# Cosine-similarity attention on one core: a third chunk of exponentials computed without ScalarE, moment statistics for Q in half of the norm groups, joint products

## The chip, the core and the metric

The kernel runs on one core of a Trainium2 chip. The metric is device time in microseconds (us), median of several runs. The core's engines work side by side, each through its own list of instructions in order, and meet at semaphores: TensorE (PE in the profile; PEld is its weight load), VectorE (DVE), ScalarE (ACT), GpSimd (POOL), and SyncE (SP), which here only issues DMAs.

## The reference

```python
Q, K, V: (8, 12, 512, 64) float32, tau = 0.1
Q_norm = Q / (norm(Q, axis=-1) + 1e-10)
K_norm = K / (norm(K, axis=-1) + 1e-10)
scores = einsum('bhqd,bhkd->bhqk', Q_norm, K_norm) / tau
weights = exp(scores - max(scores)); weights = weights / (sum(weights) + 1e-10)
return einsum('bhqk,bhkd->bhqd', weights, V)
```

Scores lie between -10 and 10, so the kernel leaves the maximum out; it gets the sum of a row's weights from a column of ones that stands beside V.

## The kernel before

The 96 heads are worked in 48 pairs of two. For a pair `s` (function `pair`, from L323, and `rest`, from L619) these operations are made, in names that the text below uses:

- **Loads** (L334, L339): Q, K and V of both heads, 128 partitions of 4 rows each. Q and K go to a ring of 15 buffers, V to one of 10.
- **Squares** (L366): GpSimd squares Q and K in one instruction of 128x1024, to bf16.
- **Sums of squares** (L393): TensorE multiplies the squares with a unit matrix, 16 matmuls of 64 columns that add up in PSUM (8 for Q, 8 for K), and VectorE reduces the 64 columns to 16 norms (L410). For the K of pairs in `BY_VECTOR`, and then the Q too, VectorE reduces the 128x512 squares itself (L418).
- **Inverse roots** (L442 to L473): for a norm group of pairs (`GROUPS`: one, two, then four pairs at a time, 19 groups) VectorE makes 1/sqrt in 8 or 9 small instructions.
- **Scaling** (L485): Q on VectorE; K on VectorE for the pairs in `K_ON_DVE`, on GpSimd for the others; 128x512 each.
- **Transposes** (L494): 8 on TensorE into one PSUM buffer, copied out by VectorE (L512).
- **Scores** (L633): for each of four chunks of 128 keys two matmuls of 512 columns, one for each head, that run beside each other on two halves of the array. Two PSUM buffers of 128x1024 take turns.
- **Exponentials** (L657): ScalarE, 128x1024 for a chunk, from PSUM to bf16.
- **Products** (L682): 32 matmuls of 65 columns with V (cast to bf16 by GpSimd, L665), in groups of four; head 0 into one PSUM bank, head 1 into another.
- **Outputs**: for each head VectorE takes the reciprocal of the four row sums (L701) and multiplies (L703), and SP stores the pair (L707). The products of the next pair may only write a bank that has been read.

Two of the 192 chunks, chunk 3 of pairs 36 and 45 (`OFF`), do without ScalarE (`poly`, L554): TensorE writes the scores of one head at a time into the transposes' PSUM buffer, VectorE splits each value into an exponent that is a bf16 bit pattern (L573) and a rest (L575), and GpSimd makes a polynomial of the rest in six instructions of 128x1024 (L601 to L604).

The order on every engine is written out by hand in `ORDER` (L814): five lists of numbers, each the place of an operation in the program's list, in which a pair's operations stand together. Each operation also carries a kind and a due time, as a planner would use them, but nothing in the file reads them: the lists alone set the order. An operation waits for those that it needs (`needs`) and, its engine being in order, so does all that stands behind it.

Of the kernel before, what the change touches and what calls it, by code (L numbers as in the profile page):

```python
# [5 lines left out]
ALU = mybir.AluOpType  # L6
# [102 lines left out]
def bass_cosine_similarity_attention_kernel(  # L109
# [200 lines left out]
    def stats(s):  # L310
        return s >= STATS_FROM and group[s] not in NORM_ON_ACT

# [10 lines left out]
    def pair(s):  # L323
# [6 lines left out]
        for w, x in ((0, Q), (1, K)):  # L330
            if s == 0:
                for h in range(2):
                    P.add(("LD", 0, w, h), "act" if w else "sp", "ldh", -1000 + h,  [],
                          lambda e, w=w, x=x, h=h: e.dma_start(out=qk[iq][:, w, h], in_=src(x, s)[:, h]), slot=f"head{w}_{h}")  # L334
                continue
            P.add(("LD", s, w), "sp", "ld1" if s == 1 else "ld", s, [*([("SCL", 0, w, 0), ("SCL", 0, w, 1), ("SQ", 0, w, 0), ("SQ", 0, w, 1)] if s == R_QK else [key("SCL", s - R_QK, w), *((squares(s - R_QK, w) if w or not stats(s - R_QK) else [("RED", s - R_QK, 0)]) if s >= R_QK else [])])],
                  lambda e, w=w, x=x: e.dma_start(out=qk[iq][:, w], in_=src(x, s)),
                  slot=f"first{s}_{w}" if s <= 3 else f"qk{iq}")
# [195 lines left out]
    def last_step(s, c):  # L534
        return 5 if (s, c) in OFF_ON_POOL + OFF_ON_BOTH else 4
# [18 lines left out]
    def poly(s, c, at):  # L554
# [4 lines left out]
        a0, a1, a2, a3, a4 = POLY_K if here else POLY  # L559
# [39 lines left out]
        if (s, c) in OFF_ON_POOL:  # L599
            k = cc ** 0.5  # L600
            steps = [("pool", "yt", mul(w, z, z)), ("pool", "ys", add(w, w, a1, k)),  # L601
                     ("pool", "ys", lambda e: e.tensor_scalar(out=z, in0=z, scalar1=a2 * cc, scalar2=a3 * cc, op0=ALU.mult, op1=ALU.add)),
                     ("pool", "yt", mul(w, w, w)), ("pool", "yt2", lambda e: e.tensor_tensor(out=w, in0=w, in1=z, op=ALU.add)),
                     ("pool", "yt3", mul(e_, w, p2))]  # L604
# [146 lines left out]
POLY = (-186.9751803485176, 100772.4799431421, -50373599.073513225, 207520169.07623482, 3.565140779347853e-11)  # L751
OFF = {(36, 3): (36, 36), (45, 3): (45, 45)}
# [8 lines left out]
BY_VECTOR = (35, 39, 43, 47)  # L761
Q_ON_PE = ()
SUM_BOTH = (4, 5, 6, 7, 8, 9, 10, 11, 12, 13, 14, 15, 16, 17, 18, 19, 20, 21, 22, 23, 24, 25, 26, 27, 28, 29, 30, 31, 32, 33, 34, 36, 37, 38, 40, 41, 42, 44, 45, 46)
# [3 lines left out]
STATS_FROM = 99  # L767
# [6 lines left out]
JOINT = False  # L774
RCPJ = ()
JOINT_FROM = 0
OFF_ON_POOL = ((36, 3), (45, 3))
OFF_ON_BOTH = ()
X_ON_POOL = ()
K_ON_DVE = (1, 2, 3, 4, 9, 12, 15, 18, 21, 24, 27, 30, 33, 36, 39, 40, 42, 44, 46, 47)  # L780
# [29 lines left out]
def slack(s, most):  # L810
# [14 lines left out]
    ),  # L825
    "pool": (
# [113 lines left out]
```

## Time and profile before

| | before |
|---|---|
| device time, median of 3 runs | 189.33 us (188.67, 189.33, 189.76) |
| span of the profiled execution | 186.8 us |
| median less that span | 2.5 us |
| ScalarE busy | 180.2 us (96%) |
| TensorE matmuls busy, weight loads busy | 179.5 us (96%), 117.9 us (63%) |
| GpSimd busy | 165.7 us (89%) |
| VectorE busy | 159.9 us (86%) |
| granted TensorE clock | 1.000 |

The span runs from the first instruction to the last of the profiled execution; the device time has what lies around it as well. Busy is the time in which an engine has at least one instruction in work. Instructions of ScalarE and VectorE overlap with the next one of the same engine, so their durations add up to more than the busy time, and what one of them costs is the step from its start to the start of the next.

### The profile page before, as it was taken

The page shows a single profiled execution, that of the slowest core. Times are in us where ns is not written, and L with a number is a line of the kernel's source. Part 1 is how long each engine was busy: PE and PEld are TensorE (multiplying, and loading weights), DVE is VectorE, ACT ScalarE, POOL GpSimd, SP SyncE. Part 2 cuts the span into 40 slices and gives each one's busy share as a digit, 9 for nine tenths or more (in the row PEclk, how much of TensorE's full clock was granted, in tenths as well). Part 3 has the DMA queues.
Part 4 walks back from the last instruction along what each step waited for, and adds up shares of the span by engine and source line. Part 5 has one row for each costly group of instructions (what it writes and reads, how often), then busy time and mean ns, then how long its engine had stood idle before and what let it go on. Part 6 is the DMA issues. An engine that isn't in the chain of part 4 may idle for free.

```text
span 186.8 us, 7242 instructions
## 1 busy us (share of the span) xinstructions
PE 179.5 (96%) x3010; PEld 117.9 (63%) x3010; DVE 159.9 (86%) x523; ACT 180.2 (96%) x210; POOL 165.7 (89%) x147
## 2 busy tenths in 40 slices
PE   7889999999999999999999999999999999998993
PEld 2456766666667666666676666766656566555653
DVE  2789998987987978979889988999999999998664
ACT  5799999999999999999999999999999999999992
POOL 3799999999989998999999899999999999907940
PEclk9999999999999999999999999999999999999999
DMA  5999999999999877999999999999798731113135
GB/s 158 354 349 351 349 358 329 288 351 364 370 376 369 283 245 230 309 303 307 312 379 367 328 371 335 319 312 298 241 303 294 239 105 56 60 56 116 60 112 168
DMA packets 52447, 50.79 MB, mean 272 GB/s; under 512 B 3136, under 2 KB 52416, under 8 KB 52416
## 3 DMA queue, kind: packets, MB, share of 16 engines
q1 hardware_dynamic: 51984, 50.02, 81.8%
q8 instruction: 23, 0.38, 0.8%
q10 hardware_dynamic: 432, 0.33, 0.5%
q14 instruction: 8, 0.07, 0.1%
HBM read 37.75 MB, written 12.58 MB: 269 GB/s over the span
## 4 chain that ended last, share of the span: by engine, by line
ACT 92%; PE 3%; DVE 2%; DMA 1%; POOL 0%; issue 0%; DVEq 0%
ACT et L657 91%; DMA qk<-in_K_dram 1%; PE oops L682 1%; PE scps L633 1%; DVE xs L260 1%; DVE ob L732 0%; POOL sq L256 0%; PE tps L283 0%; ACT ys L432 0%; DVE qn L273 0%; DVE ob L703 0%; PE oops L401 0%; ACT nps L435 0%; PE oops L281 0%; DVE rd L730 0%
## 5 line engine op out<-in xcount | busy, mean ns | idle before, releaser
L657 ACT ACTIVATE et<-scps 128x1024 bf16<-128x1024 f32 (+1 forms) x191 | 173.8, 1155 | 0.3 <-PE scps L633 0.3
L366 POOL TENSOR_TENSOR sq<-qk 128x1024 bf16<-128x1024 f32 x44 | 82.8, 1895 | 0.6 <-DMA qk<-in_K_dram 0.6
L633 PE MATMUL scps<-qt 64*128 64x512 bf16 x380 | 74.5, 386 | 2.2 <-ACT et L657 1.0
L682 PE MATMUL oops<-vb,et 128*128 128x65 bf16 x1504 | 75.8, 194 | 0.1
L682 PEld LDWEIGHTS oops<-vb,et 128*128 128x128 bf16 x1504 | 57.0, 98 | 27.7 <-issue 21.9
L485 DVE TENSOR_TENSOR qn<-qk,nps 128x512 bf16<-128x512 f32 x67 | 44.2, 678 | 0.7 <-ACT nps L435 0.6
L703 DVE TENSOR_TENSOR ob<-oops,rd 128x256 f32<-128x256 f32 x94 | 39.5, 422 | 1.7 <-DVE ys L447 0.2
L512 DVE COPY qt<-tps 128x1024 bf16<-128x1024 bf16 x47 | 32.3, 687 | 3.9 <-PE tps L494 3.0
L494 PE MATMUL tps<-ident,qn 128*128 128x128 bf16 x376 | 34.3, 220 | 0.6 <-DVE qn L485 0.6
L485 POOL TENSOR_TENSOR qn<-qk,rk 128x512 bf16<-128x512 f32 x27 | 28.1, 1045 | 2.6 <-DVE rk L443 1.7
L665 POOL TENSOR_SCALAR vb<-vf 128x512 bf16<-128x512 f32 x48 | 29.3, 629 | 0.2
L633 PEld LDWEIGHTS scps<-qt 64*128 64x128 bf16 x380 | 18.3, 92 | 16.5 <-ACT et L657 4.8
L396 PE MATMUL oops<-sq,ident 128*128 128x64 bf16 x640 | 27.6, 192 | 0.0
L494 PEld LDWEIGHTS tps<-ident,qn 128*128 128x128 bf16 x376 | 21.7, 98 | 9.4 <-issue 3.4
L396 PEld LDWEIGHTS oops<-sq,ident 128*128 128x128 bf16 x640 | 22.2, 97 | 6.1 <-issue 5.7
L701 DVE RECIPROCAL rd<-oops 128x4 f32<-128x4 f32 x94 | 16.5, 178 | 10.4 <-PE oops L682 5.2
L410 DVE TENSOR_REDUCE nps<-oops 128x16 f32<-128x64 f32 x40 | 8.7, 217 | 2.0 <-PE oops L396 2.0
L596 POOL TENSOR_TENSOR xw<-xz 128x1024 f32<-128x1024 f32 x2 | 3.8, 1895 | 5.6 <-DVE xz L575 5.6
L443 DVE SCALAR_TENSOR_TENSOR nps<-nps,ys 128x32 f32<-128x32 f32 (+3 forms) x45 | 7.9, 190 | 0.4
L195 PE MATMUL oops<-warm_in 128*128 128x512 bf16 x10 | 4.4, 631 | 1.0 <-DVE warm_in L199 1.0
L357 POOL TENSOR_TENSOR sq<-qk 128x512 bf16<-128x512 f32 (+1 forms) x5 | 4.6, 954 | 0.8 <-DMA qk<-in_K_dram 0.6
L418 DVE TENSOR_REDUCE nps<-sq 128x8 f32<-128x512 bf16 x8 | 5.3, 684 | 0.0
(64 smaller groups left out, 72.5 us busy)
## 6 DMA issues: line engine op xcount, KB each, us to landing
vf<-in_V_dram SPq DMA_DIRECT2D x48, 256.0 KB, 5.6
qk<-in_Q_dram SPq DMA_DIRECT2D x47, 256.0 KB, 4.4
qk<-in_K_dram SPq DMA_DIRECT2D x47, 256.0 KB, 5.8
out_dram<-ob SPq DMA_DIRECT2D x47, 256.0 KB, 3.8
qk<-in_Q_dram SPq DMA_DIRECT2D x2, 128.0 KB, 2.6
qk<-in_K_dram ACTq DMA_DIRECT2D x2, 128.0 KB, 2.8
out_dram<-ob SPq DMA_DIRECT2D x1, 128.0 KB, 1.9
out_dram<-ob SPq DMA_DIRECT2D x1, 64.0 KB, 1.8
```

Source lines behind the costliest of these rows:

```text
L366: lambda e: e.tensor_tensor(out=sqf, in0=data, in1=data, op=ALU.mult))
L396: last = e.matmul(out=o_ps[bank][:, 320:384], lhsT=ident[:, :], rhs=sq[iqs][:, :, 4 * k : 4 * k + 4], start=(k == 0), stop=(k == 15), skip ...
L410: lambda e, bank=bank, dst=x2[:, :, c8 : c8 + 8]: e.tensor_reduce(out=dst, in_=o_ps[bank][:, 320:384].rearrange("p (w g e) -> p w g e", w= ...
L485: lambda e, w=w, r=r: e.tensor_tensor(out=qn[iqn][:, w].rearrange("p t h d -> p h t d"), in0=qk[iq][:, w].rearrange("p h (t d) -> p h t d" ...
L494: last = e.transpose(t_ps[:, w, t, :], qn[iqn][:, w, t].rearrange("p h d -> p (h d)"), ident[:, :])
L512: lambda e, ws=ws: e.tensor_copy(out=qt[iqt][:, ws, :, :].rearrange("p w t x -> p (w t x)"), in_=t_ps[:, ws, :, :].rearrange("p w t x -> p ...
L633: last = e.matmul(out=sc_ps[:, 2 * b + h, :], lhsT=qt[iqt][64 * h : 64 * h + 64, 1, c, :], rhs=qt[iqt][64 * h : 64 * h + 64, 0, :, :], sta ...
L657: lambda e, c=c, b=b, hs=hs: e.activation(out=et[iet][:, c, hs[0] : hs[-1] + 1, :], in_=sc_ps[:, 2 * b + hs[0] : 2 * b + hs[-1] + 1, :], f ...
L665: return e.tensor_scalar(out=out, in0=in_, scalar1=1.0, scalar2=1.0, op0=ALU.mult, op1=ALU.mult)
L682: last = e.matmul(out=o_ps[h][:, 65 * t : 65 * t + 65], lhsT=et[iet][:, c, h, 128 * t : 128 * t + 128], rhs=vb[:, iq, c, h, :], start=(i = ...
L701: lambda e, hs=slice(0, 2) if s in RCPJ else hs, grid=r_all: e.reciprocal(out=rd[io][:, hs, :], in_=grid[:, :, :, DIM]))
L703: lambda e, hs=hs, grid=grid: e.tensor_tensor(out=ob[io][:, hs], in0=grid[:, :, :, 0:DIM], in1=rd[io][:, hs, :].unsqueeze(3).to_broadcast( ...
```

## The change

- Chunk 3 of pair 27 joins `OFF`: one exponential of 128x1024 less on ScalarE (187 of that size become 186), and one more chunk of `poly`.
- The polynomial's form is another one: GpSimd works five instructions for a chunk where it had six (the addition of two tensors goes).
- In the norm groups 6, 8, 10, 12, 14, 16 and 18 (22 pairs: 8, 9, 12, 13, 16, 17, 20 to 23, 28 to 31, 36 to 39, 44 to 47) the norms of Q come from `bn_stats` on VectorE (L378 to L387: four instructions for a pair, each over 128 values a partition, straight from the loaded Q), and three small instructions for a group turn mean and variance into sums of squares (L461 to L466). GpSimd squares K alone there (L363, 128x512), and TensorE sums K alone (8 matmuls). `BY_VECTOR` loses pairs 39 and 47, which are in such groups.
- `JOINT` from pair 10 on: one reciprocal and one multiplication on VectorE for both heads of a pair in place of two each, but for the pairs of `OFF` and the last one. The next pair's products into either bank then wait for the one multiplication.
- `K_ON_DVE` shrinks from 20 pairs to 12; the other eight K scalings go to GpSimd.
- The load of Q and that of K have a semaphore each.
- All five lists of `ORDER` are new, the first pairs' part nearly as it was.

```diff
     def stats(s):
-        return s >= STATS_FROM and group[s] not in NORM_ON_ACT
+        return group[s] in STATS
...
-                  slot=f"first{s}_{w}" if s <= 3 else f"qk{iq}")
+                  slot=f"first{s}_{w}" if s <= 3 else f"qk{iq}_{w}")
...
         if (s, c) in OFF_ON_POOL:
-            k = cc ** 0.5
-            steps = [("pool", "yt", mul(w, z, z)), ("pool", "ys", add(w, w, a1, k)),
-                     ("pool", "ys", lambda e: e.tensor_scalar(out=z, in0=z, scalar1=a2 * cc, scalar2=a3 * cc, op0=ALU.mult, op1=ALU.add)),
-                     ("pool", "yt", mul(w, w, w)), ("pool", "yt2", lambda e: e.tensor_tensor(out=w, in0=w, in1=z, op=ALU.add)),
-                     ("pool", "yt3", mul(e_, w, p2))]
+            steps = [("pool", "yt", mul(w, z, z)), ("pool", "ys", add(w, w, a1, cc)),
+                     ("pool", "ys", lambda e: e.tensor_scalar(out=z, in0=z, scalar1=a2, scalar2=1.0, op0=ALU.add, op1=ALU.mult)),
+                     ("pool", "yt", mul(w, w, z)), ("pool", "yt3", mul(e_, w, p2))]
...
-OFF = {(36, 3): (36, 36), (45, 3): (45, 45)}
+OFF = {(27, 3): (27, 27), (36, 3): (36, 36), (45, 3): (45, 45)}
-BY_VECTOR = (35, 39, 43, 47)
+BY_VECTOR = (35, 43)
-SUM_BOTH = (4, 5, 6, 7, 8, 9, 10, 11, 12, 13, 14, 15, 16, 17, 18, 19, 20, 21, 22, 23, 24, 25, 26, 27, 28, 29, 30, 31, 32, 33, 34, 36, 37, 38, 40, 41, 42, 44, 45, 46)
+SUM_BOTH = (4, 5, 6, 7, 10, 11, 14, 15, 18, 19, 24, 25, 26, 27, 32, 33, 34, 40, 41, 42)
-STATS_FROM = 99
+STATS = (6, 8, 10, 12, 14, 16, 18)
-JOINT = False
+JOINT = True
-JOINT_FROM = 0
-OFF_ON_POOL = ((36, 3), (45, 3))
+JOINT_FROM = 10
+OFF_ON_POOL = ((27, 3), (36, 3), (45, 3))
-K_ON_DVE = (1, 2, 3, 4, 9, 12, 15, 18, 21, 24, 27, 30, 33, 36, 39, 40, 42, 44, 46, 47)
+K_ON_DVE = (1, 2, 3, 4, 9, 12, 18, 24, 30, 36, 42, 47)
```

The five lists had 1841 numbers in all and have 1801. Four places of TensorE's new list, with what the numbers stand for:

- `984 958 1218 1219 962 1010`: scores of chunk 25.3 (pair 25, chunk 3); a product group of pair 24, both sum groups of pair 32, a product group of 24; scores of 26.0
- `1522 1461 1463 1730 1464 1465 1524`: scores of 40.0; two product groups of 38, a sum group of 46, two product groups of 38; scores of 40.1
- `1592 1692 1690 1566 1568 1569 1570 1617`: scores of 42.3; two transpose groups of 45, four product groups of 41; scores of 43.0
- `841 871 869 843 818`: scores of 21.0; two transpose groups of 22; scores of 21.1; the first product group of 20

A product group is four matmuls, a sum group eight, a transpose group four.

More of the change, by code (lines that the diff above doesn't have):

```diff
@@ L534, in last_step @@
     def last_step(s, c):
-        return 5 if (s, c) in OFF_ON_POOL + OFF_ON_BOTH else 4
+        return 4
     def exps(s, c):
@@ L558, in poly @@
         here = in_psum(s)
-        a0, a1, a2, a3, a4 = POLY_K if here else POLY
+        a0, a1, a2, a4 = POLY
         lift = LIFT_K if here else LIFT
@@ L750 @@
 LIFT = 71
-POLY = (-186.9751803485176, 100772.4799431421, -50373599.073513225, 207520169.07623482, 3.565140779347853e-11)
-OFF = {(36, 3): (36, 36), (45, 3): (45, 45)}
+POLY = (-131.77899651091911, 109622.99404139613, -167.5284161360313, -2.6307902185888065e-08)
+OFF = {(27, 3): (27, 27), (36, 3): (36, 36), (45, 3): (45, 45)}
 PIECES = ((0, 0, 4), (1, 0, 2), (1, 2, 4))
```

153 rows, old and new, of the table ORDER are left out of this document.

## The prediction

> **What bounds the kernel now.** I read the page first: its sums, then the chain that ended last.
>
> ```profile
> span 186.8 us, 7242 instructions
> PE 179.5 (96%) x3010; PEld 117.9 (63%) x3010; DVE 159.9 (86%) x523; ACT 180.2 (96%) x210; POOL 165.7 (89%) x147
> ACT 92%; PE 3%; DVE 2%; DMA 1%; POOL 0%; issue 0%; DVEq 0%
> ```
>
> ScalarE carries the chain. The chain in order of time and the waits of ScalarE say how:
>
> ```profile
> 11.89 167.82 ACT et L657 x183
> 182.94 0.42 DVE ob L703
> 183.54 0.42 DVE ob L732
> ACT et L657 <- PE scps L633: 0.3, 1, 0.3
> ```
>
> From 11.9 us to 179.7 us nothing but exponentials: 183 in 167.82 us, 0.917 us a step. One lasts 1.167 us in its group (below), so neighbours overlap by 0.25 us, and the table of waits, which lists idle time, is nearly empty. Lost time hides in the overlap. A stretch without loss gives the floor:
>
> ```profile
> L657 ACT ACTIVATE et<-scps x16: 1117/1198/1292, 119.9 to 133.5; 128x1024 bf16<-128x1024 f32 x16
> ```
>
> Sixteen starts in 13.6 us are 15 steps of 0.907 us; the first of them is a longer one, so I take 0.905 as the floor. The other 0.012 us of the mean, 183 times, are 2.2 us in which an exponential came late for want of scores. Who is late is seen in TensorE's timeline (start, length, count):
>
> ```profile
> 103.46 0.61 PE L494 MATMUL tps<-ident,qn 128*128 128x128 bf16 x8
> 104.00 0.39 PE L633 MATMUL scps<-qt 64*128 64x512 bf16 x2
> 104.32 0.54 PE L682 MATMUL oops<-vb,et 128*128 128x65 bf16 x12
> 104.79 0.39 PE L633 MATMUL scps<-qt 64*128 64x512 bf16 x2
> 105.11 0.41 PE L396 MATMUL oops<-sq,ident 128*128 128x64 bf16 x8
> 105.36 0.53 PE L682 MATMUL oops<-vb,et 128*128 128x65 bf16 x12
> ...
> 149.51 0.39 PE L633 MATMUL scps<-qt 64*128 64x512 bf16 x2
> 149.83 0.42 PE L682 MATMUL oops<-vb,et 128*128 128x65 bf16 x8
> 150.08 0.63 PE L396 MATMUL oops<-sq,ident 128*128 128x64 bf16 x16
> 150.65 0.39 PE L633 MATMUL scps<-qt 64*128 64x512 bf16 x2
> ```
>
> Starts give prices: scores 0.32 us (104.00 to 104.32); 12 products and the step back to scores 0.47, so 0.125 for a product group of four and 0.095 for the step; a sum group of eight 0.24 (105.11 to 105.36); two transpose groups 0.45 (103.46 to 104.00, less the step). From one score group to the next there are thus 0.415 us plus whatever lies between, against ScalarE's 0.905. At 149.51 two product groups and two sum groups make it 1.14. A score buffer is given back after 1.17 us and its scores are needed 1.81 us after the last start, so with 0.39 us of work and two hand-overs of 0.05 some 0.15 us of lateness costs nothing; what goes beyond it is lost.
>
> **The change part by part.** *ScalarE.* One exponential of 187 goes: -0.90 us on the path, by the floor, since the others close up only as far as their scores let them.
>
> The other engines' parts go by these groups (mean ns behind the bar):
>
> ```profile
> L657 ACT ACTIVATE et<-scps 128x1024 bf16<-128x1024 f32 x187 | 171.7, 1167 | 0.0
> L366 POOL TENSOR_TENSOR sq<-qk 128x1024 bf16<-128x1024 f32 x44 | 82.8, 1895 | 0.6 <-DMA qk<-in_K_dram 0.6
> L357 POOL TENSOR_TENSOR sq<-qk 128x512 bf16<-128x512 f32 x4 | 4.0, 1039 | 0.1
> L603 POOL TENSOR_TENSOR xw<-xw,xz 128x1024 f32<-128x1024 f32 x2 | 4.7, 2354 | 0.2
> L596 POOL TENSOR_TENSOR et<-xw,xp 128x1024 bf16<-128x1024 f32 x2 | 4.3, 2130 | 0.2
> L595 POOL TENSOR_SCALAR xw<-xw 128x1024 f32<-128x1024 f32 x2 | 2.1, 1045 | 0.2
> L485 POOL TENSOR_TENSOR qn<-qk,rk 128x512 bf16<-128x512 f32 x27 | 28.1, 1045 | 2.6 <-DVE rk L443 1.7 <-DVE nps L443 0.7 <-PE tps L494 0.2
> L485 DVE TENSOR_TENSOR qn<-qk,nps 128x512 bf16<-128x512 f32 x67 | 44.2, 678 | 0.7 <-ACT nps L435 0.6
> L703 DVE TENSOR_TENSOR ob<-oops,rd 128x256 f32<-128x256 f32 x94 | 39.5, 422 | 1.7 <-DVE ys L447 0.2
> L410 DVE TENSOR_REDUCE nps<-oops 128x16 f32<-128x64 f32 x40 | 8.7, 217 | 2.0 <-PE oops L396 2.0
> L418 DVE TENSOR_REDUCE nps<-sq 128x8 f32<-128x512 bf16 x8 | 5.3, 684 | 0.0
> L443 DVE SCALAR_TENSOR_TENSOR nps<-nps,ys 128x32 f32<-128x32 f32 x22 | 3.8, 191 | 0.2
> L260 DVE TENSOR_REDUCE xs<-sq 128x4 f32<-128x256 bf16 x4 | 1.5, 414 | 2.8 <-ACT sq L254 2.8
> L575 DVE SCALAR_TENSOR_TENSOR xz<-xp,tps 128x512 f32<-128x512 int16 x4 | 2.8, 688 | 0.1
> L573 DVE TENSOR_SCALAR xp<-tps 128x512 int16<-128x512 f32 x4 | 2.7, 682 | 0.0
> ```
>
> *GpSimd.* 22 squares of half the size: 22 x (1.04 - 1.895) = -18.8. Eight K scalings more: +8.4. A chunk's polynomial: a square 1.9, two of 1.045, a product of two tensors (2.35, as L603's addition), the last product 2.13, so 8.5; the old form has one square and one addition for that product, 1.9 more: 10.4. Three new for two old: +4.7. Sum -5.7: GpSimd falls from 165.7 to 160, and nothing there comes onto the path if its order is sound. Pair 27's polynomial ends some 9 us behind its scores; only the last product groups of pair 27 wait for it.
>
> *VectorE.* Two neighbouring rows of its timeline give the price of a step:
>
> ```profile
> 46.33 0.42 DVE L703 TENSOR_TENSOR ob<-oops,rd 128x256 f32<-128x256 f32 x1
> 46.67 0.18 DVE L443 SCALAR_TENSOR_TENSOR ts<-nps,ys 128x32 f32<-128x32 f32 x1
> ```
>
> 0.42 long, 0.34 to the next start: 0.08 of each length is overlap. No row shows `bn_stats`. For 128 values the two reductions of 64 and 256 bound it: 0.13 and 0.33 us after the overlap, 0.20 on the line between, which I take: 88 x 0.20 = +17.6 (11 to 29). Twenty-one small root steps of 0.11: +2.3. Joint: four instructions (2 x 0.18 + 2 x 0.42, less overlap: 0.87) become two (0.18 + 0.69, the latter as L485's 512 elements: 0.70), 34 times -0.17: -5.8. Eight K scalings -4.8; four vector reductions less and two small ones more -2.1; the third chunk's four steps +2.7. Sum +10 (ends +3 and +21): 160 becomes 170, still under ScalarE's 179, but not by much where it falls:
>
> ```profile
> 40.00:80.00 40.00, 39.96 (x728) 27.51 (x726) 34.16 (x127) 40.00 (x45) 38.22 (x31) 1.00 0.96 321
> 80.00:120.00 40.00, 39.96 (x704) 27.21 (x703) 35.39 (x113) 40.00 (x45) 39.15 (x36) 1.00 1.01 336
> 120.00:170.00 50.00, 48.54 (x779) 30.64 (x776) 48.05 (x142) 50.00 (x56) 43.90 (x37) 1.00 0.62 198
> ```
>
> (third busy number: VectorE.) In 40 to 120 us it is busy for 69.6 of 80; twelve pairs' statistics, the third chunk, less joint steps and K scalings put about 9 on that. The stretch behind, at 48 of 50, shows that ScalarE can be fed with VectorE so full.
>
> *TensorE.* 18 sum groups go (86 to 68): -4.3. A third chunk's scores run head by head, +0.65, in place of a score group, -0.42. From the lists, each interval between score groups summed with the prices above: 897 ns on average before, 883 after, against 905. But an average isn't what delays an exponential. By the lists, 84 intervals of 188 pass the budget before and 82 of 187 after; with lateness carried on and 0.15 us of it free, they lose 1.1 us before (the trace lost 2.2 in all) and 1.9 after. The new list has worse single places: 1.36 us at 42.3, where eight transposes and four product groups stand between two score groups, 1.14 at 40.0, 1.12 at 25.3. So +0.7, with ends -1 (the mean decides) and +1.5 (the lost time scales as counted).
>
> *Waits that the change adds.* A joint multiplication holds both banks. The next pair's products wait, and behind them on TensorE all else. Last product out 0.19, hand-over 0.05, reciprocal and step 0.21, multiplication 0.69, hand-over 0.05: 1.19 us. In the new list 24 of 33 joint pairs have two score and two transpose groups there, 2 x 0.415 + 0.45 = 1.28; six have 1.05 to 1.21; three more. Cover is there, barely, if VectorE is free at that moment; I cost it at nothing, and the third rival prices it.
>
> *End.* The list has pair 46's products ahead of the last scores, so its multiplication (182.94 above) no longer stands before the last pair's: -0.1. Loads, stores and the split semaphores are hidden: SP waits for older pairs than before nowhere near use.
>
> Sum: -0.90 + 0.70 - 0.10 = -0.3. The span goes from 186.8 to 186.5; the same 2.5 us lie around it, so the median of 189.33 goes to **189.0**. A measurement of this kernel can tell about 0.5% (0.95 us) from no change; so I forecast no change that can be told, with a range of its own of 188.4 to 190.2.
>
> **Rivals.** *Faster: TensorE's relief decides.* The distance of its mean from the budget grows from 8 to 22 ns, so its backlogs end sooner and the lost 2.2 us halve, whatever single places say: 189.33 - 0.90 - 1.1 - 0.1 = 187.2. For it: the place at 149.51 is made of the very sum groups that go in 22 pairs. Against: the count by places. TensorE's 63% of weight loads bears on this: the Trainium skill (Perfetto Trace Analysis, Identifying the Most-Contended Engine) says matmul busy time doesn't measure how near TensorE is to its limit and that weight-load busy time does; by that a third of TensorE is free, places in its list cost nothing lasting, and the gain is 0.9 at least. The timeline's steps, 0.897 of 0.905, say otherwise for this kernel.
>
> *Slower: the joint product.* VectorE runs instructions of 0.6 us, nearly without a gap. If one is still in work when a pair's last product ends, by 0.3 us on average and in one pair of three, then less the 0.09 of cover and what the freed TensorE time absorbs, 11 x 0.17 = 1.9 us come on top: 190.9. For it: no cover to speak of, and up to 29 us of `bn_stats`. Against: waits of this kind exist before and are short (total, times, longest):
>
> ```profile
> PEld oops L682 <- DVE rd L701: 2.5, 11, 0.2
> PEld oops L682 <- DVE ob L703: 1.7, 6, 0.4
> ```
>
> It decides from 1.3 us in all, 0.04 for each joint pair.
>
> *Slower: statistics shut GpSimd out.* The new reads of Q from SBUF on VectorE hold up GpSimd for their length, 22 x 0.8 = 17.6 us: -5.7 turns into +12, GpSimd stands at 178, and about 2 us come on: 191. No row before shows one engine holding up the other; L260's reduction from SBUF ran at its plain rate. The Trainium skill (SBUF — State Buffer, SBUF: two separate sides) states such a lock for VectorE instructions in a two-port mode or with two SBUF inputs, and this one has one input.
>
> **Numbers.** Forecast 0.46; TensorE's relief 0.27; joint 0.22; the lock 0.05. Faster by over 0.5% is the second, 0.27; slower the last two, 0.27; within 0.5% the forecast, 0.46. The range 187.4 to 191.0 leaves out some 0.1 on each side.
>
> **What would show it.** In the profile after: 186 large exponentials; their step at 0.915 to 0.925; `bn_stats` at 0.28 long; VectorE near 170 busy, GpSimd near 160; late exponentials around pairs 15, 25, 40 and 42. Wrong if the step falls to 0.911 or less (first rival), if products wait for VectorE's multiplication in many pairs for over 0.1 us (second), or if GpSimd's squares of 128x512 take much over 1.04 (third).

## The result, and the profile after

| | before | after |
|---|---|---|
| device time, median (22 runs each) | 189.14 us (188.65 to 191.5) | 188.3 us (187.97 to 189.8) |
| ratio, 95% interval | | 0.9948 [0.9928, 0.9967] |
| span of the profiled execution | 186.8 us | 186.4 us |
| large exponentials | 187 | 186 |

The change makes the kernel faster by 0.98 us (0.62 to 1.36 by the interval; 0.84 between the medians): just at the 0.5% that the prediction named as the least that can be told. The prediction had 189.0 in a range of 187.4 to 191.0, and the time lies in that range. It is 0.1 us under the narrower range of the forecast's own case (188.4 to 190.2), and the interval lies wholly below 1, so there is a small gain that can be told where the forecast had none.

First the page of the kernel after: the sums, then the chain's shares by engine.

```profile
span 186.4 us, 7029 instructions
PE 177.0 (95%) x2866; PEld 113.6 (61%) x2866; DVE 164.4 (88%) x556; ACT 179.3 (96%) x209; POOL 159.9 (86%) x158
ACT 92%; PE 3%; DVE 2%; DMA 1%; POOL 0%; issue 0%; DVEq 0%
```

ScalarE carries the chain as before. GpSimd has lost 5.8 us (165.7 to 159.9), VectorE has gained 4.5, TensorE has lost 2.5. The chain in order of time:

```profile
12.12 55.93 ACT et L655 x61
...
68.06 87.19 ACT et L655 x95
...
155.26 10.19 ACT et L655 x11
...
165.46 13.86 ACT et L655 x15
...
181.56 0.70 DVE ob L701
...
183.21 0.42 DVE ob L730
```

These are 182 exponentials in 167.21 us (from 12.12 to 179.33), 0.919 us each; before it was 0.917. The chain breaks into four pieces, at 68.06, 155.26 and 165.46 us: there an exponential came so late that it waited visibly. They are behind scores 15.3, 40.0 and 42.3. The prediction had priced the last two from the list; of pair 15 it had said only that exponentials would be late around it. The largest single loss, 0.256 us at 119.40 us behind scores 30.0, it had not named, and the chain doesn't break there. The third break in TensorE's timeline:

```profile
163.67 0.39 PE L631 MATMUL scps<-qt 64*128 64x512 bf16 x2
163.99 0.62 PE L494 MATMUL tps<-ident,qn 128*128 128x128 bf16 x8
164.45 0.65 PE L680 MATMUL oops<-vb,et 128*128 128x65 bf16 x16
165.03 0.39 PE L631 MATMUL scps<-qt 64*128 64x512 bf16 x2
```

From 163.67 to 165.03 are 1.36 us, the number that the prediction had worked out from the list.

Below, "lost time" is one figure for each kernel: over the large exponentials from the second on, what the step from one start to the next has above 0.904 us, the step where nothing is late (between the first and the second ScalarE has two small instructions of its own). It is 2.12 us before and 2.55 after. So the span's difference adds up from the trace: one step less, -0.904; lost time, +0.43; from the last large exponential to the end 5.45 us instead of 5.66, -0.21; the second large exponential at 12.06 instead of 11.82 us, +0.24. That is -0.45, the two spans. The last of these is no part of the change: in the runs below that point lies between 11.55 and 13.34 us, and it follows the first loads. Without it the trace gives -0.68, beside the -0.84 and -0.98 of the times.

The groups that the prediction had to estimate (busy, mean ns behind the bar), after:

```profile
L655 ACT ACTIVATE et<-scps 128x1024 bf16<-128x1024 f32 x186 | 171.0, 1131 | 0.0
L363 POOL TENSOR_TENSOR sq<-qk 128x512 bf16<-128x512 f32 x22 | 22.8, 1040 | 2.1 <-DMA qk<-in_K_dram 2.1
L383 DVE BATCH_NORM_STATS2 st<-qk 128x6 f32<-128x128 f32 x88 | 19.2, 282 | 0.0
L701 DVE TENSOR_TENSOR ob<-oops,rd 128x512 f32<-128x512 f32 x34 | 23.4, 689 | 0.2
L701 DVE TENSOR_TENSOR ob<-oops,rd 128x256 f32<-128x256 f32 x26 | 10.9, 420 | 0.1
L699 DVE RECIPROCAL rd<-oops 128x8 f32<-128x8 f32 x34 | 7.0, 206 | 7.1 <-PE oops L680 4.8 <-PE oops L396 1.2
L699 DVE RECIPROCAL rd<-oops 128x4 f32<-128x4 f32 x26 | 4.5, 175 | 2.2 <-PE oops L680 1.7 <-PE oops L396 0.4
```

### The profile page after: what moved, and what is told of

It is laid out like the page before. It is cut to its first block, busy times and chain, and to the rows that moved or that the text cites. A ratio compares the mean times of both kernels' runs of the same rounds, so it can differ in the third digit from the quotient of the medians.

```text
span 186.4 us, 7029 instructions
## 1 busy us (share of the span) xinstructions
PE 177.0 (95%) x2866; PEld 113.6 (61%) x2866; DVE 164.4 (88%) x556; ACT 179.3 (96%) x209; POOL 159.9 (86%) x158
## 4 chain that ended last, share of the span: by engine, by line
ACT 92%; PE 3%; DVE 2%; DMA 1%; POOL 0%; issue 0%; DVEq 0%
ACT et L655 91%; DMA qk<-in_K_dram 1%; PE oops L680 1%; DVE xs L260 1%; PE scps L631 1%; DVE ob L701 0%; DVE ob L730 0%; PE oops L717 0%; PE tps L283 0%; POOL sq L256 0%; ACT ys L432 0%; DVE qn L273 0%; PE scps L283 0%; ACT nps L435 0%; PE oops L281 0%
## 5 line engine op out<-in xcount | busy, mean ns | idle before, releaser
L680 PE MATMUL oops<-vb,et 128*128 128x65 bf16 x1504 | 71.1, 194 | 0.5 <-DVE ob L701 0.3
L680 PEld LDWEIGHTS oops<-vb,et 128*128 128x128 bf16 x1504 | 54.7, 98 | 26.5 <-issue 17.9
L366 POOL TENSOR_TENSOR sq<-qk 128x1024 bf16<-128x1024 f32 x22 | 41.4, 1894 | 0.4 <-DMA qk<-in_K_dram 0.2
L485 POOL TENSOR_TENSOR qn<-qk,rk 128x512 bf16<-128x512 f32 x35 | 36.0, 1044 | 6.1 <-DVE rk L443 5.4
L485 DVE TENSOR_TENSOR qn<-qk,nps 128x512 bf16<-128x512 f32 x59 | 39.2, 678 | 0.6 <-ACT nps L435 0.6
L701 DVE TENSOR_TENSOR ob<-oops,rd 128x512 f32<-128x512 f32 (+1 forms) x60 | 34.4, 573 | 0.3
L363 POOL TENSOR_TENSOR sq<-qk 128x512 bf16<-128x512 f32 x22 | 22.8, 1040 | 2.1 <-DMA qk<-in_K_dram 2.1
L699 DVE RECIPROCAL rd<-oops 128x8 f32<-128x8 f32 (+1 forms) x60 | 11.5, 193 | 9.3 <-PE oops L680 6.5
L383 DVE BATCH_NORM_STATS2 st<-qk 128x6 f32<-128x128 f32 x88 | 19.2, 282 | 0.0
L396 PE MATMUL oops<-sq,ident 128*128 128x64 bf16 x320 | 14.2, 192 | 0.0
L396 PEld LDWEIGHTS oops<-sq,ident 128*128 128x128 bf16 x320 | 11.2, 97 | 3.2 <-issue 2.5
L401 PEld LDWEIGHTS oops<-sq,ident 128*128 128x128 bf16 x224 | 8.4, 98 | 1.9 <-issue 1.4
```

What stands on the lines that cost most here:

```text
L363: lambda e: e.tensor_tensor(out=sqf[:, 8 * DIM :], in0=data[:, 8 * DIM :], in1=data[:, 8 * DIM :], op=ALU.mult))
L366: lambda e: e.tensor_tensor(out=sqf, in0=data, in1=data, op=ALU.mult))
L396: last = e.matmul(out=o_ps[bank][:, 320:384], lhsT=ident[:, :], rhs=sq[iqs][:, :, 4 * k : 4 * k + 4], start=(k == 0), stop=(k == 15), skip ...
L401: last = e.matmul(out=o_ps[bank][:, at : at + 64], lhsT=ident[:, :], rhs=sq[iqs][:, 8 * w : 8 * w + 8, 8 * k : 8 * k + 8], start=(k == 0), ...
L485: lambda e, w=w, r=r: e.tensor_tensor(out=qn[iqn][:, w].rearrange("p t h d -> p h t d"), in0=qk[iq][:, w].rearrange("p h (t d) -> p h t d" ...
L680: last = e.matmul(out=o_ps[h][:, 65 * t : 65 * t + 65], lhsT=et[iet][:, c, h, 128 * t : 128 * t + 128], rhs=vb[:, iq, c, h, :], start=(i = ...
```

## The experiments

Every kernel was timed against the kernel before on the same chip in the same rounds. The theory: the one exponential is the gain, TensorE's crowded places take part of it back, and the work moved between the other engines only makes room. The rivals: TensorE's relief is the gain; or the relief of GpSimd and VectorE is; or only the number of exponentials counts and the rest is idle.

### One exponential put back

The changed kernel with chunk 27.3 on ScalarE again, the lists adapted around it:

```diff
-OFF = {(27, 3): (27, 27), (36, 3): (36, 36), (45, 3): (45, 45)}
+OFF = {(36, 3): (36, 36), (45, 3): (45, 45)}
```

> The kernel after, with chunk 3 of pair 27 back on ScalarE (pair 27 keeps separate products); all else stays: statistics, joint products, K scalings. Theory (ScalarE's count of exponentials sets the end at 0.905 us each): +0.9, about 189.2, level with the kernel before. Rival (the relief of TensorE brought the gain, the chunk itself little): stays at 188.5 or less.

Measured: 189.09 against 189.04 us, ratio 0.9991 [0.9967, 1.0014], as the theory expected. Lost time is 2.56 us (2.55 with the chunk off), at the same places; there is one step more. So the one exponential is worth about what a step lasts, 0.8 us of the 0.98 (the difference of the two ratios; each is known to 0.4 us or so, and the trace's one step less says the same), and everything else in the change, by itself, gives nothing that can be told: GpSimd's busy time is 151.5 us here against 165.7 before, and it shows nowhere in the time.

### TensorE's sums taken away, and doubled

The kernel before with half of the sums' matmuls in 20 pairs:

```diff
-                        for k in range(8 * w, 8 * w + 8):
+                        few = s in HALF
+                        for k in range(8 * w, 8 * w + (4 if few else 8)):
```

> The kernel before, with half of the sum matmuls left out in 20 pairs (the norms are then summed over half of the dimensions): 160 matmuls, 4.6 us of TensorE, less; no other engine's work changes. Theory (late scores come from crowded places in TensorE's list): a third to half of the lost 2.2 us comes back, -0.6 to -1.1, 188.0 to 188.5. Rival (only ScalarE's count matters): unchanged, 189.1.

Measured: 188.95 against 189.04 us, 0.9995 [0.9967, 1.0023]; lost time 2.07 us against 2.12. A miss for the theory as it was put there, and the end of the rival that TensorE's relief brings the gain: 160 matmuls fewer, 2.9 us less busy time (the expectation had 4.6), and no gain. Many of the places where exponentials are late hold no sums, so the relief doesn't reach them: behind 20 products (1.04 us from scores to scores) they come late at 23.5 and 78.4 us, by 0.07 and 0.08 us, as much as in the kernel before. Some places that still hold sums are late as well.

The changed kernel with K's sums made twice in its 22 pairs:

```diff
-                    for k in range(8):
+                    for k in range(16 if stats(s) else 8):
+                        k %= 8
```

> The kernel after, with the 8 sum matmuls of K made twice in the 22 pairs with statistics (the second time over the first, the result is the same): TensorE gets back 22 x 0.23 = 5.1 us and nothing else changes. Theory (TensorE's list is a second bound close behind ScalarE): its mean interval goes from 0.883 to about 0.908 us, past the 0.905 of ScalarE, and 1.5 to 4 us come on: 190 to 192. Rival (ScalarE alone bounds; TensorE has a third to spare): 188.3 as before.

Measured: 191.63 us, 1.0123 [1.0085, 1.0161], as expected; lost time 6.02 us. This is 3.3 us over the changed kernel for 176 matmuls more. The page's sums, and the chain's shares:

```profile
PE 180.8 (95%) x3042; PEld 118.6 (62%) x3042; DVE 164.7 (87%) x556; ACT 180.4 (95%) x209; POOL 159.9 (84%) x158
PE 47%; ACT 46%; DMA 3%; DVE 2%; issue 1%; SPq 0%; DVEq 0%
```

The chain, 92% ScalarE's before, is now half TensorE's. So TensorE is a second bound right under the first: more work cost at once, and less, taken from the sums of the kernel before, brought nothing. By the weight-load measure of the Trainium skill that the prediction weighed (Perfetto Trace Analysis, Identifying the Most-Contended Engine) TensorE has over a third of its time free, its weight loads being busy 61% of the span in the changed kernel; this run, at 62%, speaks against reading that as room in this kernel.

### Exponentials left out of the kernel before

```diff
+DROP = ((8, 2), (14, 2), (20, 2), (26, 2), (32, 2), (40, 2))
...
+            if (s, c) in DROP:
+                continue
```

Once only the exponentials go:

> The kernel before, without six exponentials (chunk 2 of pairs 8, 14, 20, 26, 32 and 40; the products read what the buffer holds from an earlier pair); their scores are still made. Theory (TensorE's list paces right behind ScalarE: 0.897 us an interval against 0.905, and with two score buffers it can't run ahead): of 6 x 0.905 = 5.4 us only a part comes, -1 to -2.2, 187 to 188. Rival (ScalarE's count alone): -5.4, 183.7.

And once the scores go with them:

> As the run with six exponentials left out, but their score matmuls are left out too, 6 x 0.415 = 2.5 us of TensorE. Theory (both engines pace): 2 to 2.5 us more than that run gains, -3.3 to -4.7, 184.4 to 185.8. Rival (ScalarE's count alone): the same as with the exponentials alone.

Measured: 188.45 us, 0.9973 [0.9947, 0.9999], and 187.74 us, 0.993 [0.9904, 0.9956], both against 189.09. Six exponentials of 0.905 are 5.4 us; the first kernel gains 0.6 and the second 1.4, 0.1 and 0.2 us for each. Both are misses even for the theory: the first was expected at 1 to 2.2, the second at 3.3 or more. The rival, that only the number of exponentials counts, is out too: it had 5.4 for the first, and the same for both. The first has a fault that its expectation had not seen. Its TensorE and ScalarE at the second of the six (chunk 14.2), from two answers of the timeline:

```profile
61.67 0.39 PE L635 MATMUL scps<-qt 64*128 64x512 bf16 x2
61.99 0.41 PE L396 MATMUL oops<-sq,ident 128*128 128x64 bf16 x8
62.24 0.28 PE L686 MATMUL oops<-vb,et 128*128 128x65 bf16 x4
62.46 0.39 PE L635 MATMUL scps<-qt 64*128 64x512 bf16 x2
```
```profile
57.45 4.84 ACT L661 ACTIVATE et<-scps 128x1024 bf16<-128x1024 f32 x5
62.89 2.04 ACT L661 ACTIVATE et<-scps 128x1024 bf16<-128x1024 f32 x2 [0.60 <-PE scps L635]
```

The scores at 62.46 go into the buffer that the exponential which ended at 62.29 had held, since the two buffers take turns; then come 0.39 us of scores and two hand-overs of 0.05. So ScalarE must stand still for at least 0.49 of the 0.60 us seen, however fast TensorE is. In the second kernel the chunk uses no buffer, and what is left is that TensorE comes late. At chunk 40.2:

```profile
155.48 0.39 PE L637 MATMUL scps<-qt 64*128 64x512 bf16 x2
155.80 0.66 PE L686 MATMUL oops<-vb,et 128*128 128x65 bf16 x16
156.73 0.64 PE L396 MATMUL oops<-sq,ident 128*128 128x64 bf16 x16 [0.28 <-POOL sq L366]
157.31 0.39 PE L637 MATMUL scps<-qt 64*128 64x512 bf16 x2
```

1.83 us from scores to scores: the work of two intervals lies there, and a wait for GpSimd's squares on top. The chain's shares of the second kernel:

```profile
PE 54%; DVE 19%; ACT 13%; POOL 6%; DMA 3%; issue 2%; SPq 0%; DVEq 0%; POOLq 0%
```

ScalarE has fallen from 92% to 13%. An exponential is therefore not worth 0.9 us by itself. In these two kernels every list of the other engines stays as it was, but for the scores left out in the second, so the work of the interval has nowhere else to go. In the change it has: the lists are written anew around chunk 27.3, and there the exponential is worth about 0.8 us. That the room found elsewhere makes this difference is read from these timelines; no run shows it by itself.

### GpSimd's squares left whole

The changed kernel, but GpSimd squares Q and K in the 22 pairs, as before (with the waits for Q's load and for both halves of the buffer that belong to it):

```diff
-                  lambda e: e.tensor_tensor(out=sqf[:, 8 * DIM :], in0=data[:, 8 * DIM :], in1=data[:, 8 * DIM :], op=ALU.mult))
+                  lambda e: e.tensor_tensor(out=sqf, in0=data, in1=data, op=ALU.mult))
```

> The kernel after, with GpSimd squaring Q as well in the 22 pairs with statistics (nobody reads those squares): GpSimd gets back 22 x 0.855 = 18.8 us, 160 becomes 179 busy, and nothing else changes. Theory (without that relief GpSimd has no room for the third polynomial): K scalings and casts come late, +1 to +4 against the kernel after, 189.3 to 192. Rival (GpSimd's 26 idle us absorb it): 188.3.

Measured: 199.72 us, 1.0563 [1.0526, 1.0601]: the direction was right, the size nearly three times the upper end of what was expected (1 to 4 us). Page and waits:

```profile
PE 177.5 (90%) x2866; PEld 113.5 (57%) x2866; DVE 164.8 (83%) x556; ACT 181.0 (92%) x209; POOL 178.2 (90%) x158
POOL 42%; PE 15%; ACT 14%; issue 10%; DMA 8%; DVE 5%; SPq 3%; POOLq 0%; DVEq 0%
```
```profile
ACT et L655 <- PE scps L631: 10.0, 15, 1.8
PEld tps L494 <- POOL qn L485: 5.2, 5, 2.1
PEld oops L401 <- POOL sq L363: 4.4, 6, 1.1
```

GpSimd is busy for 178.2 us, less than ScalarE, and yet the run costs 11.4 us over the changed kernel: transposes wait for its K scalings and sums for its squares, each time at the head of TensorE's list, with scores queued behind. The sum over the whole span hides how full GpSimd is, because it has less to do at both ends. From 20 to 160 us, where all 22 squares of the changed kernel start, the windows of the changed kernel and of this one read (the last of the five busy numbers is GpSimd's, the one ahead of it ScalarE's):

```profile
20.00:160.00 140.00, 137.83 (x2325) 90.35 (x2324) 133.52 (x469) 139.99 (x154) 130.27 (x124) 1.00 0.91 303
20.00:160.00 140.00, 129.55 (x2154) 84.05 (x2150) 125.18 (x442) 132.08 (x143) 138.34 (x113) 1.00 0.88 293
```

The changed kernel leaves GpSimd 9.7 us free there, and the whole squares ask for 18.8 us more: 9.1 us too much by the plain sum, an estimate that accounts for most of the 11.4. In this run GpSimd is busy for 138.3 of the 140 us and ScalarE for 132.1, so GpSimd is the bound of that stretch; where the other 2.3 us come from is open. In the kernel before GpSimd was busy for 136.8 us of the same stretch, and the 3.2 us left are less than one more polynomial (8.5 by the prediction's sum). The moment statistics are thus what the change's other moves to GpSimd (the third polynomial, eight scalings) need.

### No joint products

```diff
-JOINT = True
+JOINT = False
```

> The kernel after with two reciprocals and two multiplications a pair again, at the places of the joint ones. Theory (the joint product's hold on both banks is covered by the order of TensorE's list): within 0.3 us of the kernel after, 188.0 to 188.6. Rival 1 (the hold costs on the path): 187.8 or less. Rival 2 (VectorE is nearly full and needs the 6 us that joint products save): 189 or more.

Measured: 190.6 us, 1.008 [1.0052, 1.0108], a miss for the theory, and what its second rival had said: 2.3 us over the changed kernel, lost time 4.70 us. Two groups, and from the page the chain's shares:

```profile
L680 PE MATMUL oops<-vb,et 128*128 128x65 bf16 x1504 | 72.1, 194 | 3.0 <-DVE ob L701 2.1 <-POOL et L596 0.3
L701 DVE TENSOR_TENSOR ob<-oops,rd 128x256 f32<-128x256 f32 x94 | 39.7, 422 | 1.5
```
```profile
DVE 37%; PE 30%; ACT 27%; issue 2%; DMA 1%; DVEq 0%
```

Products now stand still for 3.0 us, 2.1 of them for VectorE's multiplication (0.5 and 0.3 in the changed kernel), and VectorE carries more of the chain than any other engine. Its busy time is 169.8 us. So the joint form, which the prediction had as a possible cost, pays for the statistics on VectorE. One reservation: the lists are made for the joint form, and a list made for halves might do better.

### The crowded places loosened

First three places at once, at scores 4.0, 15.1 to 15.3 and 42.3, products and sums put one place on or back:

```diff
-SSQ7.1 PV2.03 SCO4.1 TR5.1
+SSQ7.1 SCO4.1 PV2.03 TR5.1
...
-SCO42.3 TR45.1 TR45.0 PV41.03 PV41.11 PV41.12 PV41.13 SCO43.0 SCX45.0 SCO43.1
+SCO42.3 TR45.1 TR45.0 SCO43.0 PV41.03 PV41.11 PV41.12 PV41.13 SCO43.1 SCX45.0
```

(The lists hold numbers; here they are by name: SCO scores, SCX scores of half a chunk by `poly`, TR transposes, SSQ sums, PV products: pair, then head and group.)

> The kernel after with three crowded places of TensorE's list loosened: a product group of pair 2 goes behind the scores of 4.1; before 15.3 the product groups of pair 14 move one place ahead; at 42.3 the scores of 43.0 go right behind the transposes, and pair 45's scores for the polynomial one place later. Theory (single places over the budget lose what lateness they leave): 0.14 + 0.14 + 0.24 us come back, 187.7 to 187.9, and the late exponentials at 24.9, 68.1 and 165.5 us of the trace are gone. Rival (the lateness only moves to the next place): 188.3.

Measured: 188.67 us, 0.9969 [0.9948, 0.9991] of before, so not under the changed kernel's 188.3; lost time 3.16 us. A miss: the exponentials at 24.9 and 165 us are no longer late, but the one at 67.8 still is (0.21 us), and so are others at 29 to 31 us, at 170 to 171 and at 179.

Next, six sum groups moved out of crowded intervals, over one score group into the light interval behind (and, in the second of these kernels, product groups at 42.3 as well). On VectorE three multiplications now stand ahead of the moved sums' reductions:

```diff
-PV10.03 SSQ15.0 SSQ15.1 PV10.13 SCO12.0 TR13.1
+PV10.03 SSQ15.0 PV10.13 SCO12.0 SSQ15.1 TR13.1
```

> The changed kernel with six sum groups (7.1, 15.1, 22.1, 30.1, 36.1, 46.1) moved one place each: out of a crowded interval between two score groups, over the next score group, into the light interval behind it. No product group changes its place, so the joint products' gaps stay; on VectorE three reductions stand behind the multiplication they stood ahead of. Theory (single crowded places are what the new list still loses, 2.55 us in all): the late exponentials near 24.9, 53.2, 68.1, 97.3, 119.4 and 155.3 us go, 0.136 + 0.155 + 0.210 + 0.124 + 0.256 + 0.212 = 1.09 us at most, less what the lighter intervals pass on: lost time 1.5 to 1.9 us, 187.3 to 187.7 against 188.3. Rival (the lateness only moves to the next place, because VectorE's and GpSimd's lists pace TensorE anyway, as the earlier loosening of three places seemed to show): lost time 2.3 us or more, 188.1 to 188.7.

> The kernel with the six moved sum groups, and at the most crowded place, behind scores 42.3, the last product group of pair 41 moved behind the first joint half-chunk of scores of 45, and the first two product groups of pair 42 moved one interval later, so that the gap for the joint multiplication stays. Theory of places: the interval of 1.36 us becomes 1.24 us, another 0.12 us of the 0.244 us lost there goes: 187.2 to 187.6. Rival (product groups, unlike sum groups, meet the wait for VectorE's multiplication wherever they are put): no change against the kernel with the sums alone, or up to 0.3 us slower.

Measured: 190.99 us, 1.01 [1.0063, 1.0137], and 191.2 us, 1.0112 [1.0085, 1.0139]. Both are slower than the kernel before: the wrong sign, and the first is outside its rival too (188.1 to 188.7). The second, 0.2 us over the first, is what its own rival had said of the product groups. The moved group 15.1 in the first of them, from the timeline of all engines (release of an idle time in brackets):

```profile
53.54 0.41 PE L396 MATMUL oops<-sq,ident 128*128 128x64 bf16 x8
...
53.99 0.21 DVE L699 RECIPROCAL rd<-oops 128x8 f32<-128x8 f32 x1 [0.45 <-PE oops L396]
...
54.23 0.69 DVE L701 TENSOR_TENSOR ob<-oops,rd 128x512 f32<-128x512 f32 x1
...
54.98 0.43 PE L680 MATMUL oops<-vb,et 128*128 128x65 bf16 x8 [0.15 <-DVE ob L701]
```

The reciprocal waits for the sums. In the code a pair's sums are put into a product bank (`attached`), behind the last products there, and the reciprocal of that bank needs them (L698). A joint reciprocal reads both banks and so waits for both banks' sums. Whatever sum stands behind the pair's last product holds the multiplication, and with it the next pair's first products. This would explain the crowded places of the new list: the sums must stand before the joint reciprocal, and behind it must come some 1.2 us without products, so heavy intervals stand ahead of light ones. Over the prices of the timeline, products behind transposes stood still for 2.1 us in all in this kernel. That isn't the whole loss: three exponentials at 27.6 to 30.9 us, 0.93 us late together, stand ahead of the first joint pair. Ahead of the first of them, the scores at 27.19 us wait for VectorE's copy of the transposes.

The check on that: five of the sums moved in the same way (7.1, the early one, stays in its place), and the five pairs in whose banks they are put (10, 14, 22, 28, 38) no longer joint, the head without the moved sum first.

```diff
-    return JOINT and s >= JOINT_FROM and s not in {i for i, _ in OFF} and s < 47
+    return JOINT and s >= JOINT_FROM and s not in (10, 14, 22, 28, 38) and s not in {i for i, _ in OFF} and s < 47
```

> The changed kernel with five of the six sum groups moved over the next score group, as in the run before (15.1, 22.1, 30.1, 36.1, 46.1; 7.1 stays), but with the five pairs whose banks these sums use (10, 14, 22, 28, 38) no longer joint: on VectorE the head whose bank holds no moved sum gets its reciprocal and multiplication first, the other head behind the sum. Theory (the joint reciprocal has to wait for the sums of both banks, so a sum group put behind its pair's last product holds the multiplication and the next pair's first products; a pair by halves does not): the waits of transposes to products, 2.1 us in the run before, go; the late exponentials near 53, 68, 97, 119 and 155 us go as well, 0.155 + 0.210 + 0.124 + 0.256 + 0.212 = 0.96 us, VectorE gets 5 x 0.17 us more; lost time 1.5 to 2.0 us, 187.3 to 187.9. Rival (the next products wait for VectorE or for the sums' reduction anyway, or the lateness moves on): lost time as in the changed kernel or more, 188.1 to 190.5.

Measured: 188.7 us, 0.9989 [0.9971, 1.0007]. The same stretch in this kernel, TensorE alone:

```profile
52.81 0.41 PE L396 MATMUL oops<-sq,ident 128*128 128x64 bf16 x8
53.06 0.38 PE L494 MATMUL tps<-ident,qn 128*128 128x128 bf16 x4
53.38 0.39 PE L631 MATMUL scps<-qt 64*128 64x512 bf16 x2
53.70 0.40 PE L494 MATMUL tps<-ident,qn 128*128 128x128 bf16 x4
53.94 0.47 PE L680 MATMUL oops<-vb,et 128*128 128x65 bf16 x8
```

The wait is gone here (0.24 us from the transposes to the products where it was 0.55), and over the kernel products behind transposes stand still for 0.65 us instead of 2.1: the mechanism holds. The time is the rival's (188.1 to 190.5), a miss for the theory's 187.3 to 187.9: lost time is 3.13 us, the late exponential near 53 us has gone, but new ones stand at 57 to 61 us (four, 0.40 us together) and others have grown. Lateness moves on. The late exponentials at 27 to 31 us are gone too, but for 0.05 us, now that the sum 7.1 is back in its place, so not all of the time from 191 us down to 188.7 is the mechanism's. Four kernels tried to take the crowded places' loss back, and none did, so what these places cost is read from the trace alone and not shown by a run; whether any list for this set of operations would lose less is open.

## Why the prediction was right, and where it was off

The bound, the count and the mechanism held: ScalarE's chain, one step of 0.905 less, and part of it given back where TensorE's new list is crowded. That the gain came out just clear of the noise and not just inside it lies in the sizes. By the letter of its three cases, 0.52% falls to the case that it gave to TensorE's relief (chance 0.27); the mark that it had set for that case, a step of 0.911 us or less, isn't there: the step is 0.919, in the 0.915 to 0.925 of its own case. Point by point:

- **One exponential, -0.90.** Right: one step in the trace, 0.8 us when it is put back. But the reason given ("the others close up only as far as their scores let them") is stronger than it was taken: without room on TensorE an exponential left out gave 0.1 to 0.2 us.
- **TensorE's places, +0.70.** The mis-sized term: +0.43 measured (2.12 to 2.55 us). The places that it had priced were there, 1.36 us to the hundredth at 42.3, and exponentials were late behind each: 0.24 us at 42.3 and 0.21 at 40.0, but only 0.06 at 25.3. Around pair 15, named without a price, 0.21 us went at 68.06. What failed was to add up places: by the count the kernel before lost 1.1 us, where the trace had 2.1, and no step of it more than 0.16. In the new list four steps lose over 0.2 us each, 0.92 together, and all the others 1.63, 0.49 less than before (42 of 184 steps lose over 8 ns, 49 of 185 before). The count, which lets 0.15 us go free, sees the four and not what the others lose less.
- **The end, -0.10.** -0.21, and not for the reason given: pair 46's multiplication stands on the chain still, at 181.56 us, now longer (0.70), but ahead of the last pair's products and not behind them.
- **GpSimd, 160.** 159.9, with squares at 1.040 us as estimated. That nothing of it comes onto the path holds only with the relief: the run with whole squares shows what hung on it. The last rival's price, 2 us for a GpSimd at 178 us, was far too low: at 178.2 the run cost 11.4. And the sum over the whole span hid how little room GpSimd had: between 20 and 160 us it had 3.2 of 140 us free in the kernel before.
- **VectorE, 170.** 164.4. `bn_stats` was as estimated, 0.282 long and 19.2 us in all. The joint form was mis-sized: reciprocals and multiplications of the pairs go from 16.5 + 39.5 to 7.0 + 4.5 + 23.4 + 10.9 us of busy time, -10.2 where the prediction took -5.8. A part of the gap is only that it had taken overlap off and these sums have not; counted from start to start, as it did, a pair goes from 1.00 to 0.75 us, some -8.4 over 34 pairs. It took 0.08 us of overlap off each instruction, but a multiplication waits for its reciprocal and doesn't overlap with it: the joint pair at 53.99 above, in the kernel with moved sums, takes 0.24 us from the one's start to the other's, more than the reciprocal's 0.21.
- **The joint wait, nothing.** Right in sum: weight loads of products waited for the multiplication 3.7 us in 16 times after, 1.7 in 6 before, but the matmuls themselves 0.3 us. The mark set for this rival, waits of over 0.1 us in many pairs, thus shows on the weight loads alone.

```profile
PEld oops L680 <- DVE ob L701: 3.7, 16, 0.3
```

- **Rivals.** TensorE's relief as the gain: refuted by halving the sums of the kernel before, no change that can be told. The slower joint form: the other way round, it is worth 2.3 us here. The lock on GpSimd: no sign, the squares of 128x512 took 1.040 us, 1.039 for the same form before, and the 12 of the 22 that ran beside a `bn_stats` (1.036 to 1.042) were no longer than the other 10 (1.038 to 1.046). This agrees with the Trainium skill (SBUF — State Buffer, SBUF: two separate sides), which has the lock only for VectorE's two-port modes and two SBUF inputs.

So the forecast lay 0.7 us above the measurement: 0.27 from the places, 0.1 from the end, 0.2 because the kernel before measured 189.14 this time and not 189.33, and the remaining 0.15 between one profiled execution (-0.68 without the first loads) and the medians (-0.84).

## What to carry to other kernels

In a kernel like this one, whose engines all stand at 86% or more, an instruction taken off the longest engine can't be counted at its length unless the others' work of that interval finds room elsewhere; price the relief of the other engines as what makes the gain possible, not as a gain, and an overload of one of them by the stretch in which its work has to be done, not by its sum over the whole span. A fused step on one engine ties together everything that its inputs had apart (here both banks' sums), and that fixes the order on the others. Single crowded places can be found exactly from prices in the timeline, but what they cost together was not had here by adding them up.

## What was not expected of the hardware

- TensorE at 113.6 us of weight loads in 186.4 is as good as full here: 176 more matmuls of 64 columns, 3.8 us of busy time, cost 3.3 us.
- A `bn_stats` over 128 values a partition takes 0.282 us, and 0.20 us from start to start: a row of the timeline of VectorE after has four in 0.88 us, three steps and a length.

```profile
50.87 0.88 DVE L383 BATCH_NORM_STATS2 st<-qk 128x6 f32<-128x128 f32 x4
```
